# A decoder layer on one core: the first modulation's weights in three transfers, its last block taken into the column sums, and the squares of x's last rows ahead of a copy

## The chip, the cores and the metric

The kernel runs on one core of a Trainium2 chip. The metric is the device time of one execution in microseconds, lower is better. Two numbers appear: the time of an execution, and the span of a profiled execution, from the first to the last instruction that the profiler recorded.

## The reference, cut to what matters

The layer takes x (512 rows of 1024) and a condition vector c of 1024. Its start, which is what the change touches:

```python
mod = jax.nn.silu(c) @ w_ada + b_ada
shift, scale, gate = jnp.split(mod, 3, axis=-1)
h = rms_norm(x, norm_gain) * (1 + scale[:, None, :]) + shift[:, None, :]
proj = h @ w_in
```

`rms_norm` divides each row by the root of the mean of its squares and multiplies by a gain. `proj` then feeds a sliding-window attention group (A) and a native sparse attention group (B) with compressed, selected and window branches; both are gated by SiLU(z), joined, multiplied by `w_out`, gated and added to x.

## The kernel before, in words

The 1024 columns of h are worked through as 8 tiles of 128 (k = 0 to 7), and the 512 rows as 4 blocks of 128 (tb). For each k the kernel needs a shift and a scale for its 128 columns. It then forms h transposed (columns on partitions), splits it into a high and a low part (hh, hl), splits the weights likewise (swh, swl in the profile), and adds three products, `first_proj(k, 0..2)` at L309 and L310, into six PSUM banks (`pj_q` sq0 to sq3, `pj_kv` skv0 and skv1).

Before the first of these products (k = 0) the following happens, in an order written out by hand: the whole stretch stands in `with in_order(tc)`, which fixes each engine's order of instructions to that of the program. Names are those of the code; the profile drops the numbers behind them.

- SyncE (SP) issues the loads: x0 (the first 128 rows of x with small inputs), three more blocks of x, then the modulation weights of k = 0 (`load_ada(0)`, L221, `ada_ring`), the projection weights of k = 0 (`load_wst`, L225, `wst_ring`), and the same for k = 1 to 3 with a small transfer for the bias lines (L331) between. Each issue takes a place on this queue; from the ninth on an issue waits until the eighth before it has landed.
- TensorE turns x by 128 x 128 transposes into PSUM (`x_turned`, L341); VectorE (L372, L373) and, for the last block, ScalarE (L382, L383) copy the result to `xTp`. For block 2 the second half goes through the bank `pj_q[0]`. Dummy matmuls with zeros (`dummies`, L336) stand between; unless told otherwise they write `pj_q[0]`.
- ScalarE squares and sums the rows of x (L371, L376) and VectorE does so for half of the last block (L377). L379, L380 and `rsqrt` (L102 to L109) make the reciprocal roots, `rx`. They are transposed and spread over the partitions (L393, bank `rbp`), and `scaled` (L293) multiplies them into the turned x.
- The modulation of k = 0: `mod_pe` (L237) multiplies SiLU(c), eight columns of 128, with the weights: for each half e four blocks c, block 4e + c of the inputs, into four groups of 32 rows of the bank `pm`, of which one row each is not zero. ScalarE copies `pm` to `macc` (L241). `mod_col` (L247) sums over the rows with a column of ones into `pc`. `mod_ab` (L252, L253) makes shift and scale (AB) of it. `dummies(ND[3])`, two of them, stand between the two halves, and two more behind `mod_col`.
- ScalarE makes the projection weights' high part (`weights_high`, L285) and then h in three pieces (L404). The first L309 needs both.

The banks `pm`, `rbp` and `pc` are taken in this order from one pool of two buffers:

```python
ps_pj = ctx.enter_context(tc.tile_pool(name="ps_pj", bufs=2, space=PSUM))
```

The order around the modulation:

```python
first_mod = mod_pe(0)
next(first_mod)
dummies(ND[3])
for _ in first_mod:
    pass
rbp = ps_pj.tile([128, 512], F32, name="pj")
```

Behind this stage a loop over k runs the products while the next k's modulation, h and weights are made, and the attention and the output projection follow.

Of the kernel before, what the change touches and what calls it, by code (L numbers as in the profile page):

```python
# [19 lines left out]
S, D, HD, NB = 512, 1024, 64, 4  # L20
# [11 lines left out]
ND = (9, 0, 1, 2)  # L32
# [50 lines left out]
def hybrid_layer_kernel(ctx, tc, A, out):  # L83
    nc = tc.nc
    PE, DVE, ACT, POOL, SP = nc.tensor, nc.vector, nc.scalar, nc.gpsimd, nc.sync
# [12 lines left out]
    def rsqrt(v, n):  # L98

        y = sm.tile([128, n], F32, name="n_y")  # L100
        t = sm.tile([128, n], F32, name="n_t")
        DVE.tensor_scalar(y.bitcast(I32), v.bitcast(I32), -0.5, float(MAGIC), op0=OP.mult, op1=OP.add)  # L102
        DVE.tensor_tensor(t, y, y, op=OP.mult)
        DVE.scalar_tensor_tensor(t, t, -0.375 * NEWTON[0], v, op0=OP.mult, op1=OP.mult)
        DVE.scalar_tensor_tensor(y, t, 0.375 * NEWTON[0] * NEWTON[1], y, op0=OP.add, op1=OP.mult)
        DVE.tensor_tensor(t, y, y, op=OP.mult)
        DVE.scalar_tensor_tensor(t, t, 64.0 / 9.0, v, op0=OP.mult, op1=OP.mult)
        DVE.scalar_tensor_tensor(t, t, -10.0 / 3.0, t, op0=OP.add, op1=OP.mult)
        DVE.scalar_tensor_tensor(y, t, 5.0, y, op0=OP.add, op1=OP.mult)  # L109
        return y  # L110
# [13 lines left out]
    cT, prm, ident = first[:, 0:8], first[:, 8:40], first[:, 40:168]  # L124
# [8 lines left out]
    ones = con.tile([128, 1], F32, name="ones")  # L133
# [13 lines left out]
    sc_col = con.tile([128, 8], F32, name="sc_col")  # L147
# [66 lines left out]
    ada, wst = {}, {}  # L214
# [2 lines left out]

    def load_ada(k):
        ada[k] = ada_ring[:, k % NR]
        for e in range(2):  # L220
            SP.dma_start(ada[k][:, e], A["w_ada_ss"][k][:, e])  # L221

# [5 lines left out]
    macc, pcs = {}, {}  # L228
# [3 lines left out]
    def mod_pe(k):  # L232

        pm = ps_pj.tile([128, 512], F32, name="pj")[:, 0:256]
        for e in range(2):
            for c in range(4):
                PE.matmul(pm[32 * c:32 * c + 32, :], scz[:, 4 * e + c, :], ada[k][:, e, 256 * c:256 * c + 256],  # L237
                          start=e == 0, stop=e == 1, skip_group_check=True)
            yield
        macc[k] = stp.tile([128, 2, 128], F32, name="macc", bufs=2)  # L240
        ACT.activation(macc[k].rearrange("p a b -> p (a b)"), pm, AF.Copy)  # L241

    def mod_col(k):

        pc = pcs[k] = ps_pj.tile([128, 512], F32, name="pj")
        for s in range(2):
            PE.matmul(pc[:, s:s + 1], macc[k][:, s, :], ones, start=True, stop=True)  # L247

    def mod_ab(k):

        pc = pcs.pop(k)
        DVE.tensor_tensor(AB[:, k, 1:2], pc[:, 0:1], prm[:, k:k + 1], op=OP.add)  # L252
        DVE.scalar_tensor_tensor(AB[:, k, 0:1], pc[:, 1:2], prm1[:, k:k + 1], prm[:, 24 + k:25 + k],  # L253
                                 op0=OP.add, op1=OP.mult)
# [11 lines left out]
    pj_q = [spb.tile([128, 512], F32, name=f"sq{tb}") for tb in range(4)]  # L266
    pj_kv = [spb.tile([128, 2, 256], F32, name=f"skv{p}") for p in range(2)]
    flat_kv = [t.rearrange("p a b -> p (a b)") for t in pj_kv]
# [21 lines left out]
    def scaled(k, by, parts=(slice(0, S),)):  # L290
        y[k] = xT[k]
        for c in parts:
            DVE.tensor_tensor(y[k][:, c], xT[k][:, c], by[:, c], op=OP.mult)  # L293
# [19 lines left out]
    halves = (slice(0, 256), slice(256, 512))  # L313
    quarters = tuple(slice(128 * t, 128 * t + 128) for t in range(NB))

    with in_order(tc) as begun:
# [6 lines left out]
        for tb in range(1, NB):  # L323
            SP.dma_start(xn[:, tb], A["xn"][tb - 1])
        load_ada(0)
        load_wst(0)
        for k in range(1, NR):
            load_ada(k)
            load_wst(k)
            if k == 2:  # L330
                SP.dma_start(bl[0:48, :], A["bias"])  # L331
        DVE.memset(scz, 0.0)

        def dummies(n, bank=pj_q[0]):
            for _ in range(n):
                PE.matmul(bank, zero[:, 0:128], zero, start=True, stop=True)  # L336

        def x_turned(tb, bank, half=0):
            for k in range(4):
                c = 128 * (4 * half + k)  # L340
                PE.transpose(bank[:, 128 * k:128 * k + 128], xn[:, tb, c:c + 128], ident)  # L341

        def x_kept(tb, bank, half=0):
            return xTp[:, 4 * half:4 * half + 4, 128 * tb:128 * tb + 128], bank.rearrange("p (k q) -> p k q", k=4)
# [12 lines left out]
        def silu_rows(g):  # L357
            for j in range(4):
                PE.transpose(flat_kv[g][:, 128 * j:128 * j + 128],
                             sc_col[:, 4 * g + j:4 * g + j + 1].to_broadcast([128, 128]), ident)  # L360

        for tb in range(NB):
            dummies(ND[tb] if 0 < tb < 3 else 0, flat_kv[1])
            x_turned(tb, pj_q[tb])
            if tb < 3:
                x_turned(tb, (flat_kv[0], pj_q[3], pj_q[0])[tb], 1)
            if tb == 2:
                for g in range(2):
                    silu_rows(g)
            if tb < 3:  # L370
                ACT.activation(sqs, xn[:, tb], AF.Square, scale=1.0 / 32, accum_out=ss[:, tb:tb + 1])  # L371
                DVE.tensor_copy(*x_kept(tb, pj_q[tb]))  # L372
                DVE.tensor_copy(*x_kept(tb, (flat_kv[0], pj_q[3], pj_q[0])[tb], 1))  # L373
        x_turned(3, pj_q[2], 1)
        sx = con.tile([128, NB], F32, name="sx")
        ACT.activation(sqs[:, 0:512], xn[:, 3, 0:512], AF.Square, scale=1.0 / 32, accum_out=ss[:, 3:4])  # L376
# [2 lines left out]
        DVE.tensor_scalar(sx[:, 0:3], ss[:, 0:3], EPS, None, op0=OP.add)  # L379
        DVE.scalar_tensor_tensor(sx[:, 3:4], ss[:, 3:4], EPS, ss[:, 4:5], op0=OP.add, op1=OP.add)  # L380
        rx = rsqrt(sx, NB)
        ACT.activation(*x_kept(3, pj_q[3]), AF.Copy)  # L382
        ACT.activation(*x_kept(3, pj_q[2], 1), AF.Copy)  # L383
        for g in range(2):
            ACT.activation(scb[:, 512 * g:512 * g + 512], flat_kv[g], AF.Copy)
# [3 lines that stand above are left out]
        for _ in first_mod:  # L389
            pass  # L390
        rbp = ps_pj.tile([128, 512], F32, name="pj")
        for tb in range(NB):
            PE.transpose(rbp[:, tb * 128:(tb + 1) * 128], rx[:, tb:tb + 1].to_broadcast([128, 128]), ident)  # L393
        mod_col(0)
        dummies(ND[3])
        scaled(0, rbp, halves[0:1])
        mod_ab(0)
        scaled(0, rbp, halves[1:2])
        scaled(1, rbp)
# [33 lines left out]
        for k in range(8):  # L433
            if k + NR < 8:
                load_ada(k + NR)
                load_wst(k + NR)
            if k == LW - 1:
                SP.dma_start(rest[:, 0:960], A["rest"])
                for _ in range(5):
                    load_next()  # L440
            first_proj(k, 0)
            if k + 1 in PE_MOD:
                for _ in mod_pe(k + 1):
                    pass
            first_proj(k, 1)
            if k + 1 in PE_MOD:
                mod_col(k + 1)
            if k == 2:
                bank = ps_pj.tile([128, 512], F32, name="pj")
                bias_lines(bank)  # L450
            if k < 7:
                new_tile(k + 1)
            if k == 2:
                ACT.activation(lsb, bank[0:64, 0:320], AF.Copy)
                for a in range(2):
                    for b in range(2):
                        SP.dma_start(line_d[a, :, 320 * b:320 * b + 320], lsb[32 * b + 8 * a:32 * b + 8 * a + 8, :])
            first_proj(k, 2)
            if k == 7:
                split_to("kv_cmp", 3, 0)  # L460
# [38 lines left out]
    def PJ():  # L499
        n_pj[0] += 1  # L500
        return (ps_px if n_pj[0] % 3 == 0 else ps_pj).tile([128, 512], F32, name="pj")
# [577 lines left out]
    for n in range(8):  # L1079
# [3 lines left out]
        for c in halves if n == 7 else (slice(0, S),):  # L1083
            b = PJ()[:, 0:c.stop - c.start]
# [78 lines left out]
```

## Time and profile before

| what | us |
| --- | --- |
| median of three runs | 306.17 |
| the three runs | 306.03, 306.17, 306.64 |
| the profiled execution, its own time | 306.96 |
| its span | 305.2 |

A row of a timeline gives the start in us from the span's start, the time in us, engine, line, operation, what is written and what is read, and how many instructions are merged; in brackets stands the idle time of the engine before it and what ended that. PE is TensorE, PEld its weight loads, DVE VectorE, ACT ScalarE, SPq the queue that issues transfers. A matmul of 32-bit floats shows as two records: eight records of L237 are four matmuls. A row of the waits gives who waited for whom, the total in us, how often, and the longest.

### The profile page before, as it was taken

Reading aid. Unit: us, or ns where it says so; the run is one execution under the profiler, and the core shown is the slowest. Engines: PE = TensorE matmul, PEld = TensorE weight load, DVE = VectorE, ACT = ScalarE, POOL = GpSimd, SP = SyncE. Lnnn points to the kernel's source line nnn. Section 1 sums busy time; section 2 is a strip of 40 time slices with the busy share of each in tenths; the row PEclk is TensorE's granted clock in tenths of the full one; section 3 lists DMA queues with packets and bytes.
Section 4 is the critical chain, followed back from the end, with each engine's and each line's share of the span. In section 5 each row is a group of like instructions: output and inputs, shape, how many; then the busy total and the mean of one; then the engine's idle time right before and its main releaser. Section 6 shows DMA issues by size and latency. Waiting matters only on the chain.

```text
span 305.2 us, 5838 instructions
## 1 busy us (share of the span) xinstructions
PE 295.9 (97%) x2119; PEld 252.4 (83%) x2119; DVE 238.7 (78%) x668; ACT 195.6 (64%) x474; POOL 4.7 (2%) x26
## 2 busy tenths in 40 slices
PE   8999999999999999999999999999999999989994
PEld 4677888889989999989787887888888888868884
DVE  3899996999985587977999999999978958555321
ACT  4876547777975579958696677759767847623100
POOL 1000000000100000000000000000000000000000
PEclk9999999999999999999999999999999999999998
DMA  7999957893475650410815030545400000008331
GB/s 270 378 375 409 337 192 257 256 275 122 140 213 168 207 174 2 126 49 0 273 40 207 2 103 34 210 146 198 131 12 0 0 2 1 2 10 244 92 103 37
DMA packets 27420, 44.21 MB, mean 145 GB/s; under 512 B 1712, under 2 KB 19408, under 8 KB 27392
## 3 DMA queue, kind: packets, MB, share of 16 engines
q1 hardware_dynamic: 27392, 43.84, 42.9%
q8 instruction: 17, 0.28, 0.4%
q14 instruction: 11, 0.09, 0.1%
HBM read 41.70 MB, written 2.14 MB: 144 GB/s over the span
## 4 chain that ended last, share of the span: by engine, by line
PE 76%; DVE 10%; ACT 6%; DMA 3%; issue 2%; SPq 1%; ACTq 0%
PE pj L522 30%; PE sq L309 8%; PE po L1010 8%; PE s L932 6%; PE pj L512 6%; PE pt L993 4%; PE skv L310 4%; PE pt L983 3%; DMA ada_ring<-in_w_ada_ss 3%; PE s L639 2%; DVE wl L191 2%; DVE qs L572 1%; ACT qs L571 1%; DVE pa L940 1%; ACT pa L947 1%
## 5 line engine op out<-in xcount | busy, mean ns | idle before, releaser
L190 ACT ACTIVATE wh<-raw 128x512 fp32r<-128x512 f32 (+1 forms) x52 | 31.7, 632 | 22.1 <-PE pj L522 20.6
L191 DVE TENSOR_TENSOR wl<-raw,wh 128x512 fp32r<-128x512 f32 (+1 forms) x52 | 35.1, 692 | 6.8 <-ACT wh L190 6.4
L512 PE MATMUL pj<-wl,hh 128*128 128x256 f32 (+1 forms) x128 | 37.0, 289 | 0.0
L512 PE MATMUL pj<-wh,hh 128*128 128x256 f32 (+1 forms) x128 | 36.5, 287 | 0.0
L512 PE MATMUL pj<-wh,hl 128*128 128x256 f32 (+1 forms) x128 | 36.3, 285 | 0.0
L947 ACT ACTIVATE pp<-pp,nm 128x256 f32<-128x256 f32 (+2 forms) x48 | 29.3, 611 | 7.2 <-DVE nm L940 7.0
L522 PE MATMUL pj<-hh,wh 128*128 128x512 f32 x80 | 32.2, 403 | 0.0
L522 PE MATMUL pj<-hl,wh 128*128 128x512 f32 x80 | 31.9, 399 | 0.0
L522 PE MATMUL pj<-hh,wl 128*128 128x512 f32 x80 | 31.6, 395 | 0.0
L940 DVE CUSTOM_DVE_ANT_0 pp<-s,bias 128x256 f32<-128x256 f32 (+2 forms) x48 | 25.9, 552 | 2.2 <-PE s L932 1.7
L522 PE MATMUL pj<-yh,wh 128*128 128x512 f32 (+1 forms) x72 | 26.2, 373 | 1.3 <-ACT yh L869 1.3
L522 PE MATMUL pj<-yh,wl 128*128 128x512 f32 (+1 forms) x72 | 26.9, 373 | 0.0
L522 PE MATMUL pj<-yl,wh 128*128 128x512 f32 (+1 forms) x72 | 26.9, 373 | 0.0
L1010 PE MATMUL po<-ptT,xf 128*64 128x128 f32 x432 | 25.3, 274 | 0.0
L1010 PEld LDWEIGHTS po<-ptT,xf 128*64 128x64 f32 x432 | 23.5, 137 | 1.5 <-issue 0.9
L512 PEld LDWEIGHTS pj<-wl,hh 128*128 128x128 f32 x128 | 24.1, 188 | 0.3 <-issue 0.2
L512 PEld LDWEIGHTS pj<-wh,hl 128*128 128x128 f32 x128 | 24.1, 188 | 0.3 <-issue 0.3
L512 PEld LDWEIGHTS pj<-wh,hh 128*128 128x128 f32 x128 | 24.1, 189 | 0.2 <-issue 0.2
L932 PE MATMUL s<-kTb,qs 128*128 128x256 f32 (+2 forms) x96 | 23.5, 357 | 0.0
L968 DVE TENSOR_SCALAR pp<-pp,rr,xf 128x256 f32<-128x256 f32 (+2 forms) x48 | 21.2, 477 | 0.5
L994 ACT COPY ptT<-pt 128x384 f32<-128x384 f32 (+1 forms) x32 | 16.2, 524 | 4.7 <-PE pt L993 3.1
L947 ACT ACTIVATE pa<-pa,nm 128x257 f32<-128x257 f32 (+1 forms) x32 | 15.2, 476 | 4.1 <-DVE nm L940 4.1
(241 smaller groups left out, 676.0 us busy)
## 6 DMA issues: line engine op xcount, KB each, us to landing
ada_ring<-in_w_ada_ss SPq DMA_DIRECT2D x16, 512.0 KB, 10.0
raw<-in_w_cmp SPq DMA_DIRECT2D x8, 512.0 KB, 5.3
raw<-in_w_gate SPq DMA_DIRECT2D x8, 512.0 KB, 4.4
raw<-in_w_o SPq DMA_DIRECT2D x8, 512.0 KB, 4.6
wst_ring<-in_w_qkv_a SPq DMA_DIRECT2D x8, 384.0 KB, 9.7
xr<-in_xT SPq DMA_DIRECT2D x8, 256.0 KB, 3.1
bias<-line_d SPq DMA_DIRECT2D x8, 256.0 KB, 3.9
raw<-in_w_q_b SPq DMA_DIRECT2D x4, 512.0 KB, 5.1
```

The source lines that it names most:

```text
L190: ACT.activation(wh, src, AF.Copy)
L191: DVE.tensor_tensor(wl, src, wh.bitcast(F32), op=OP.subtract)
L309: PE.matmul(pj_q[tb], lt, w[:, 0:512], start=f, stop=l, skip_group_check=True)
L310: PE.matmul(pj_kv[tb // 2][:, tb % 2, :], lt, w[:, 512:768], start=f and tb % 2 == 0, stop=l, skip_group_check=True)
L512: PE.matmul(bank[:, t * n:(t + 1) * n], h[:, tb * 128:(tb + 1) * 128], w[:, k % 2, :], start=k == 0 and m == 0, stop=k == 7 and m == 2)
L522: PE.matmul(bank, w, h[:, cols], start=k == 0 and m == 0, stop=k == 7 and m == 2)
L932: PE.matmul(ps[g], qs[h][:, 128 * i:128 * i + 128], kT[br, g][:, hl_, lo:lo + n], start=hl_ == 0, stop=hl_ == 1)
L940: DVE.tensor_tensor_reduce(out=P[:, g, 0:w], in0=ps[g][:, 0:w], in1=bt, scale=1.0, scalar=init, op0=OP.add, op1=OP.min, accum_out=nm[:, g: ...
L947: ACT.activation(P[:, g, 0:e], P[:, g, 0:e], AF.Exp, bias=nm[:, g:g + 1], scale=-1.0, accum_out=dn[:, g:g + 1])
L968: DVE.tensor_scalar(v, v, rr[:, g:g + 1], gates[:, g, br:br + 1], op0=OP.mult, op1=OP.mult)
L994: ACT.copy(T[:, 0:nb, :], rev(pt[:, 0:nb * 128].rearrange("p (b q) -> p b q", b=nb)))
L1010: PE.matmul(o[64 * g:64 * g + 64, 128 * i:128 * i + 128], vb[:, 64 * g:64 * g + 64], sl["T"][g][:, b, :], start=first_of and b == 0, stop= ...
```

## The change

The modulation weights of k = 0 come in three transfers instead of two: columns 0 to 1024 (half 0), 1024 to 1792 (three blocks of half 1) and 1792 to 2048 (its last block). The row products leave out the last block. `mod_col(0)` multiplies it with its column of SiLU(c) straight into the column sums, ahead of the sums of `macc`. The root's transposes are split: two blocks and the first half of `scaled` stand before `mod_col(0)`, two blocks after, and one dummy fewer follows. The copy of block 2's second half out of `pj_q[0]` moves behind `rsqrt`, so VectorE's squares of x's last rows come before it.

```diff
     def load_ada(k):
         ada[k] = ada_ring[:, k % NR]
+        if k == 0:
+            flat = lambda t: t.rearrange("p a b -> p (a b)")
+            for lo, hi in ((0, 1024), (1024, 1792), (1792, 2048)):
+                SP.dma_start(flat(ada[k])[:, lo:hi], flat(A["w_ada_ss"][k])[:, lo:hi])
+            return
         for e in range(2):
             SP.dma_start(ada[k][:, e], A["w_ada_ss"][k][:, e])
...
         for e in range(2):
-            for c in range(4):
+            for c in range(3 if e and k == 0 else 4):
                 PE.matmul(pm[32 * c:32 * c + 32, :], scz[:, 4 * e + c, :], ada[k][:, e, 256 * c:256 * c + 256],
                           start=e == 0, stop=e == 1, skip_group_check=True)
...
         pc = pcs[k] = ps_pj.tile([128, 512], F32, name="pj")
+        for s in range(2 if k == 0 else 0):
+            PE.matmul(pc[:, s:s + 1], ada[k][:, 1, 768 + 128 * s:896 + 128 * s], sc_col[:, 7:8], start=s == 0, stop=False,
+                      skip_group_check=True)
         for s in range(2):
-            PE.matmul(pc[:, s:s + 1], macc[k][:, s, :], ones, start=True, stop=True)
+            PE.matmul(pc[:, s:s + 1], macc[k][:, s, :], ones, start=k > 0, stop=True, skip_group_check=True)
...
                 DVE.tensor_copy(*x_kept(tb, pj_q[tb]))
-                DVE.tensor_copy(*x_kept(tb, (flat_kv[0], pj_q[3], pj_q[0])[tb], 1))
+                if tb < 2:
+                    DVE.tensor_copy(*x_kept(tb, (flat_kv[0], pj_q[3])[tb], 1))
...
         rx = rsqrt(sx, NB)
+        DVE.tensor_copy(*x_kept(2, pj_q[0], 1))
         ACT.activation(*x_kept(3, pj_q[3]), AF.Copy)
...
         rbp = ps_pj.tile([128, 512], F32, name="pj")
-        for tb in range(NB):
-            PE.transpose(rbp[:, tb * 128:(tb + 1) * 128], rx[:, tb:tb + 1].to_broadcast([128, 128]), ident)
+
+        def root_turned(tbs):
+            for tb in tbs:
+                PE.transpose(rbp[:, tb * 128:(tb + 1) * 128], rx[:, tb:tb + 1].to_broadcast([128, 128]), ident)
+
+        root_turned((0, 1))
+        scaled(0, rbp, halves[0:1])
         mod_col(0)
-        dummies(ND[3])
-        scaled(0, rbp, halves[0:1])
+        root_turned((2, 3))
+        dummies(ND[3] - 1)
         mod_ab(0)
         scaled(0, rbp, halves[1:2])
         scaled(1, rbp)
```

## The prediction

> **What bounds the kernel now.** I read the page's first part, then the chain of work that ended last in order of time, then the timeline of each engine between 8 and 17 us, where the edited lines run, and last who waited for whom on TensorE.
>
> ```profile
> span 305.2 us, 5838 instructions
> PE 295.9 (97%) x2119; PEld 252.4 (83%) x2119; DVE 238.7 (78%) x668; ACT 195.6 (64%) x474; POOL 4.7 (2%) x26
> ```
>
> The chain in order of time, from the weights of the first modulation to the first matmul of the projection:
>
> ```profile
> 3.35 8.41 DMA ada_ring<-in_w_ada_ss
> 11.80 0.64 PE pj L237 x8
> 12.44 0.58 PE pj L393 x4
> 13.02 0.59 PE pj L247 x4
> 13.96 0.50 ACT hh L404
> 14.50 0.50 PE sq L309
> ```
>
> Behind 14.50, TensorE's waits up to 60 us come to one entry, the one that ends there:
>
> ```profile
> PE sq L309 <- ACT hh L404: 0.4, 1, 0.4
> ```
>
> So the start waits on data, and from 14.5 us the kernel is a stream of matmuls almost without holes. A microsecond won or lost before 14.5 us therefore arrives at the end nearly whole. The question is when the first L309 starts. Before it stand: the weights land (11.76 by the chain), the second half of the row products (L237), ScalarE's copy of them (macc), the column sums (L247), two small VectorE steps (L252, L253), h (L404).
>
> TensorE and ScalarE there:
>
> ```profile
> 11.14 0.60 PE L336 MATMUL sq<-zero 128*128 128x512 bf16 x2
> 11.80 0.64 PE L237 MATMUL pj<-ada_ring,scz 128*32 128x256 f32 x8
> 12.37 0.65 PE L393 MATMUL pj<-xf,n_y 128*128 128x128 f32 x4
> 12.99 0.61 PE L247 MATMUL pj<-ones,macc 128*128 128x1 f32 x4
> ...
> 9.10 0.63 ACT L376 ACTIVATE sq_both<-xf 128x512 f32<-128x512 f32 x1
> 9.63 0.19 ACT L376 ACTIVATION_READ_ACCUMULATOR sq_both<-xf 128x1 f32 x1
> ...
> 11.18 1.09 ACT L385 ACTIVATE xf<-skv 128x512 f32<-128x512 f32 x2
> 12.56 0.38 ACT L241 ACTIVATE macc<-pj 128x256 f32<-128x256 f32 x1 [0.28 <-PE pj L237]
> 12.84 0.83 ACT L285 ACTIVATE swh<-wst_ring 128x768 fp32r<-128x768 f32 x1
> 13.96 0.88 ACT L404 ACTIVATE hh<-xTp,AB 128x128 fp32r<-128x128 f32 x2 [0.28 <-DVE AB L253]
> ```
>
> VectorE there:
>
> ```profile
> 9.14 0.68 DVE L373 COPY xTp<-sq 128x512 f32<-128x512 f32 x1
> 9.73 0.68 DVE L377 CUSTOM_DVE_ANT_0 sq_both<-xf 128x512 f32<-128x512 f32 x1
> ...
> 10.53 0.16 DVE L380 SCALAR_TENSOR_TENSOR sx<-ss 128x1 f32<-128x1 f32 x1
> ...
> 12.11 0.16 DVE L109 SCALAR_TENSOR_TENSOR n_y<-n_t,n_y 128x4 f32<-128x4 f32 x1
> 13.06 0.42 DVE L293 TENSOR_TENSOR xTp<-xTp,pj 128x256 f32<-128x256 f32 x1 [0.79 <-PE pj L393]
> 13.64 0.16 DVE L252 TENSOR_TENSOR AB<-pj,xf 128x1 f32<-128x1 f32 x1 [0.15 <-PE pj L247]
> 13.71 0.21 DVE L253 SCALAR_TENSOR_TENSOR AB<-pj,prm,xf 128x1 f32<-128x1 f32 x1
> 13.84 1.01 DVE L293 TENSOR_TENSOR xTp<-xTp,pj 128x256 f32<-128x256 f32 x2
> ```
>
> **The change part by part.**
>
> *The squares ahead of the copy.* The copy at 9.14 leaves its place and L377 takes it: x's last rows are there (ScalarE squares them from 9.10), and the ScalarE sum that L380 needs ends at 9.82. So L377 and all behind it move up by 9.73 - 9.14 = 0.59: L109 starts at 11.52 and ends at 11.68. The copy follows, 0.08 before L109's end by the overlap of neighbours that don't depend on each other (13.71 + 0.21 against 13.84), so from 11.60 to 12.28. VectorE's next work, L293, starts later than that before and after, so VectorE itself loses nothing.
>
> *Who waits for the moved copy.* It reads the PSUM bank `pj_q[0]`, and the two dummy matmuls between the halves of the first modulation write that bank by default (`sq<-zero` at 11.14). Before, the copy ended at 9.82, long ahead of 11.14. Now it ends at 12.28, it stands ahead of the dummies in the program, and a matmul that overwrites a bank waits for its reader, as elsewhere in this trace:
>
> ```profile
> PEld pt L993 <- ACT ptT L994: 0.3, 1, 0.3
> ```
>
> TensorE's order is fixed, so the second half of the products, the transposes of the root and the column sums are queued behind the dummies. From the end of a VectorE step to TensorE it is 0.10 (L109 ends at 12.27, L393 starts at 12.37): dummies from 12.38 to 12.98.
>
> ```profile
> 16.07 0.28 PE L310 MATMUL skv<-swh,hh 128*128 128x256 f32 x1
> 16.27 1.07 PE L237 MATMUL pj<-ada_ring,scz 128*32 128x256 f32 x16
> ```
>
> L237 here starts 0.08 before the full-width matmul ahead of it ends, so the second half starts at 12.90 instead of 11.80: 1.10 later. Bounds: 12.80 if a dummy only holds the array for its stream, and 13.00 if the copy starts after L109 has ended. I take 12.90, since L310 then L237 is the same pair of shapes.
>
> *Three blocks of four.* Sixteen records take 1.07 and eight 0.64, so one is 0.054 and six take 0.53: the products end at 13.43 (bounds 0.38 less or 0.64). ScalarE's copy follows by 0.12 as before (12.44 to 12.56): macc from 13.55 to 13.93. ScalarE had the L385 copies until 12.27, so that is no longer what it waits on. The weights' high part (0.83) follows until 14.66 and is hidden until h is due.
>
> *Root transposes first, then the sums.* Four take 0.65; two, 0.12 apart, 0.41. They run from 13.35 to 13.76, inside the wait for macc, and release the first half of L293 at 13.80, which ends at 14.22. Hidden, since h needs AB later than that.
>
> *The last block into the column sums.* The column sums as records:
>
> ```profile
> L247 PE MATMUL pj<-ones,macc x8: 166/250/271, 13.0 to 19.0; 128*128 128x1 f32 x8
> ```
>
> Two matmuls of this form are added, four records, spaced (0.61 - 0.25) / 3 = 0.12. Written to run before macc is there, they can't: the tile `pc` is the third from a pool of two buffers, so it takes the bank of `pm`, which macc is copied from. They wait for that copy (13.93), and L247 starts 0.05 after it (12.94 to 12.99), at 13.98. Eight records instead of four then take 0.25 + 7 x 0.12 = 1.09 and end at 15.07 instead of 13.60. Bounds: 14.60 if the four direct ones were hidden ahead of macc, and 15.20 if the four cost a whole 0.61 more.
>
> *Behind them.* L252 starts 0.04 after the sums: 15.11 instead of 13.64; L253 and h follow as before: h at 15.43, first L309 at 15.97. The other two transposes, 0.41, end by 15.4 and the second half of L293 starts some 0.07 late, which its reader covers: the third L404 piece comes two pieces, 0.88, after the first. One dummy fewer saves nothing, since the two ran while L309 waited for h.
>
> *Three transfers instead of two.* The queue that issues transfers, SyncE's:
>
> ```profile
> 2.87 0.96 SPq L221 DMA_DIRECT2D ada_ring<-in_w_ada_ss  x2
> 3.88 0.44 SPq L225 DMA_DIRECT2D wst_ring<-in_w_qkv_a  x1
> ...
> 10.54 0.33 SPq L225 DMA_DIRECT2D wst_ring<-in_w_qkv_a  x1
> 11.84 0.34 SPq L331 DMA_DIRECT2D raw<-in_bias  x1
> 12.74 2.15 SPq L221 DMA_DIRECT2D ada_ring<-in_w_ada_ss  x2
> ```
>
> One issue more is 0.48 on this queue, covered by the 8.4 us between issue and landing. The steps at 10.54, 11.84 and 12.74 are each let go by the landing of the eighth transfer before, so the landings lie 1.30 (512 KB) and 0.90 (384 KB) apart: the extra transfer shows no gap of its own. At that pace the 384 KB piece lands near 11.5 and the last 128 KB near 11.85, both long before 12.90 and 13.98. The next five issues now wait for one transfer earlier in the line, the last of them (bias) at about the old time; their data are used from 16.3 us on, later now, so nothing is exposed. If it were, a late weight stalls ScalarE first.
>
> The Trainium skill, page "DMA: Bandwidth & Descriptors", gives each transfer a fixed cost of about 2 us, mostly the receipt of the last byte. These landings, 0.90 and 1.30 apart, show no such gap between queued transfers. Were it paid in series, the first projection weights would land near 14.7, their high part end near 15.6 instead of 14.66, and the sum would be 0.15 us more.
>
> **The sum.** 15.97 - 14.50 = +1.47 us: +1.10 (dummies wait) - 0.11 (six records for eight) + 0.48 (direct matmuls behind macc). This is made against the profiled execution, 306.96 us with its span of 305.2; the median of the runs is 306.17, 0.79 below it, and 306.17 + 1.47 = 307.6. Ends of the terms: (1.00 - 0.26 + 0) = +0.74 and (1.20 + 0 + 0.60) = +1.80, so 306.9 to 308.0.
>
> **The rivals.**
>
> *The dummies don't wait (not slower).* The point is whether the copy ends before TensorE reaches them at 11.14; by the chain above it ends at 12.28, so it would need to be 1.1 us earlier, or the bank's reader not waited for. Then the second half starts at the end of the dummies, 11.66, ends at 12.20, macc starts when ScalarE is free at 12.28 (0.28 earlier than before) and ends at 12.66, and eight records end at 13.80 against 13.60: +0.2, or with the direct ones ahead of macc 13.32 and -0.28. That is 305.9 to 306.4. For it: nothing in the rows; against it: the program's order and the bank. Chance 0.13.
>
> *The direct matmuls are hidden ahead of macc.* Dummies wait, bank free: +0.99, 307.2. For it: rows don't show bank reuse here. Chance 0.12.
>
> *TensorE's clock falls.* A hole opens from 11.2 to 12.4, and the column sums are tiny.
>
> ```profile
> 1.23 4.02 PE L336 MATMUL sq<-zero 128*128 128x512 bf16 x9 [1.23 <-DVE ada_ring L320]
> ...
> 300.56 0.28 PE L522 MATMUL pj<-yh,wl 128*128 128x256 f32 x1
> ...
> 302.00:303.00 1.00, 0.00 (x0) 0.00 (x0) 0.00 (x0) 0.00 (x0) 0.00 (x0) 1.00 0.35 124
> 303.00:304.00 1.00, 0.00 (x0) 0.00 (x0) 0.00 (x0) 0.00 (x0) 0.00 (x0) 0.50 0.04 7
> ```
>
> At the end TensorE stops at 300.84 and the granted clock is 0.50 from 303.0, after 2.2 us of rest. Nine dummies took 4.02 at the start, 0.45 each, and two took 0.60 later. The new hole is 1.2 us, with 0.22 and then 0.25 us more within the next 3 us. If it is enough, some 2 to 3.4 us of matmuls behind 15.97 run at half speed and cost 1.0 to 1.7 more: 308.6 to 309.3. Chance 0.10.
>
> The Trainium skill, page "TensorE: Matmul & The Clock Gate", Part 1, says that the clock is halved after an idle window of about 3.4 us. By it the hole is too short; the trace's end shows that 2.2 us of rest can do, so the case keeps its chance.
>
> *A late small transfer or a late weight.* Up to another 0.8 on the sum, 308.4. Chance 0.05.
>
> **How the numbers follow.** The forecast itself has 0.60. A difference within 0.2%, 0.6 us, is about what this kernel's runs can't tell from none (306.03 to 306.64). Slower by more than that: forecast, hidden direct matmuls, clock, late transfer, 0.87, less 0.02 for a sum at its lower end in a low run: 0.85. The first rival and that 0.02 make 0.15, of which 0.03 stand beyond the bound on the faster side (its -0.28 with the spread of the runs) and 0.12 within it. Range: forecast and second rival (0.72) lie in 306.9 to 308.0; upward it takes in the late transfer and half of the clock case, to 309.0; it leaves out the first rival. With 0.1 for the spread of runs: 306.8 to 309.0.
>
> **What would show it.** Right: the L336 pair between the two L237 groups starts near 12.4 and names the L391 copy of xTp as what it waited for; second L237 group, six records, at 12.9; macc at 13.55; L247 and the direct matmuls together behind macc, ending near 15.1; first L309 near 16.0; L109 near 11.5; the span about 306.7. Wrong: dummies still at 11.14; direct matmuls ahead of macc; a granted clock of 0.50 after 12 us; or new waits of L309 behind 16 us that give time back or add to it.

## The result, and the profile after

The changed kernel takes 307.62 us in the median (306.72 to 309.64, eight executions) and the kernel before 305.99 (305.49 to 306.64, eight): a ratio of 1.0062, 95% interval 1.0035 to 1.0088. It is slower, by about 1.6 us.

That median stands between two groups. Each execution has a mean granted TensorE clock. Four executions of the changed kernel have 1.000 and take 306.72 to 307.29 (median 306.89). The other four have 0.991 to 0.994 and take 307.94 to 309.64 (median 308.81). An interval of 3.41 us at half speed gives a mean of 1 - 1.71 / 305 = 0.994, and the end of an execution can add to it. The 81 executions of the kernel before that were timed beside the experiments have 0.996 or more. So two things are to be explained: about 0.9 us in every execution, and about 1.9 us in half of them.

The profile shown is of an execution with a full clock: its own time is 306.72, its span 304.9. That span is a little shorter than the 305.2 of the profile before, although the first product comes later in it; the part on the prediction says where the difference goes. First the span and the engines of the page, then TensorE's timeline from the dummies to the first product, VectorE's and ScalarE's. The lines have moved: L336 is L344, L237 is L242, L393 is L405, L247 is L252 (direct) and L255 (macc), L404 is L419, L309 is L317. Two dummies stand in the program where the first row shows one; the other left no record.

```profile
span 304.9 us, 5843 instructions
PE 295.2 (97%) x2119; PEld 251.9 (83%) x2120; DVE 238.8 (78%) x668; ACT 195.5 (64%) x474; POOL 4.7 (2%) x26
```

```profile
12.22 0.38 PE L344 MATMUL sq<-zero 128*128 128x512 bf16 x1 [0.87 <-DVE xTp L391]
12.75 0.63 PE L242 MATMUL pj<-ada_ring,scz 128*32 128x256 f32 x6
13.31 0.43 PE L405 MATMUL pj<-xf,n_y 128*128 128x128 f32 x2
13.92 0.60 PE L252 MATMUL pj<-sc_col,ada_ring 128*128 128x1 f32 x4 [0.18 <-ACT macc L246]
14.39 0.58 PE L255 MATMUL pj<-ones,macc 128*128 128x1 f32 x4
15.88 0.50 PE L317 MATMUL sq<-swh,hh 128*128 128x512 f32 x1 [0.42 <-ACT hh L419]
...
9.04 0.68 DVE L386 CUSTOM_DVE_ANT_0 sq_both<-xf 128x512 f32<-128x512 f32 x1
11.40 0.16 DVE L109 SCALAR_TENSOR_TENSOR n_y<-n_t,n_y 128x4 f32<-128x4 f32 x1
11.49 0.69 DVE L391 COPY xTp<-sq 128x512 f32<-128x512 f32 x1
15.01 0.16 DVE L260 TENSOR_TENSOR AB<-pj,xf 128x1 f32<-128x1 f32 x1 [0.81 <-PE pj L255]
...
13.48 0.38 ACT L246 ACTIVATE macc<-pj 128x256 f32<-128x256 f32 x1 [1.25 <-issue]
15.33 0.88 ACT L419 ACTIVATE hh<-xTp,AB 128x128 fp32r<-128x128 f32 x2 [0.73 <-DVE AB L261]
```

The root's last step starts 0.71 us sooner (11.40 against 12.11), and nothing profits: the moved copy runs from 11.49 to 12.18, and the first row names it as what the dummies waited for, 0.87 us. The second row products start at 12.75 instead of 11.80, the direct matmuls wait for macc, and the first product starts at 15.88 instead of 14.50.

### The profile page after: what moved, and what is told of

Same layout as the page of the kernel before. It is cut to its first block, busy times and chain, and to the rows that moved or that the text cites. A ratio compares the mean times of both kernels' runs of the same rounds, so it can differ in the third digit from the quotient of the medians.

```text
span 304.9 us, 5843 instructions
## 1 busy us (share of the span) xinstructions
PE 295.2 (97%) x2119; PEld 251.9 (83%) x2120; DVE 238.8 (78%) x668; ACT 195.5 (64%) x474; POOL 4.7 (2%) x26
## 4 chain that ended last, share of the span: by engine, by line
PE 76%; DVE 12%; ACT 6%; issue 2%; DMA 2%; SPq 0%; ACTq 0%
PE pj L537 30%; PE sq L317 8%; PE po L1025 8%; PE s L947 6%; PE pj L527 6%; PE pt L1008 4%; PE skv L318 4%; PE pt L998 3%; PE s L654 2%; DMA xf<-in_xn 2%; DVE wl L191 2%; DVE qs L587 1%; ACT qs L586 1%; DVE pa L955 1%; ACT pa L962 1%
```

## The experiments

All times are compared with the kernel before on the same chip. "First product" is the start of the first L309 or L317 in the profiled execution. It moves by half a microsecond from one execution to the next with the landing of the weights (14.50 and 14.01 in two profiles of the kernel before), so the path is read by its steps, and the time by medians. The step used below goes from the start of the second row products to the first product: 14.50 - 11.80 = 2.70 us before, 15.88 - 12.75 = 3.13 in the changed kernel.

**The copy alone.** The kernel before, with one edit:

```diff
-                DVE.tensor_copy(*x_kept(tb, (flat_kv[0], pj_q[3], pj_q[0])[tb], 1))
+                if tb < 2:
+                    DVE.tensor_copy(*x_kept(tb, (flat_kv[0], pj_q[3])[tb], 1))
...
         rx = rsqrt(sx, NB)
+        DVE.tensor_copy(*x_kept(2, pj_q[0], 1))
```

> The kernel before, with the moved copy as the only edit. Theory (dummies wait): dummies near 12.3, second L237 group of eight near 12.85, first product near 15.5, 1.0 us behind before; 306.9 in executions at full clock, and part of the executions 1.7 us above that with a lower granted clock. Rival (the copy's place is harmless, the rest of the change costs): within 0.3 us of before, one clock.

Measured: 307.13 us (306.73 to 307.53, six) against 305.90, ratio 1.0042 (1.0025 to 1.0058). TensorE's timeline:

```profile
12.33 0.38 PE L336 MATMUL sq<-zero 128*128 128x512 bf16 x1 [1.16 <-DVE xTp L383]
12.85 0.64 PE L237 MATMUL pj<-ada_ring,scz 128*32 128x256 f32 x8
15.55 0.50 PE L309 MATMUL sq<-swh,hh 128*128 128x512 f32 x1 [0.45 <-ACT hh L406]
```

The wait is there, 1.16 us, the second products start 1.05 later than in the first profile of before and so does the first product; the step between them is 2.70, as before. The move alone makes the kernel slower. But none of its six executions has a clock below 1.000, although its hole on TensorE is longer than the changed kernel's. The second half of the expectation fell.

**The dummies in a free bank.** The changed kernel with

```diff
-        dummies(ND[3])
+        dummies(ND[3], pj_q[1])
```

between the halves.

> The changed kernel, with the two dummies between the halves of the first modulation written to a bank whose readers are long done (sq1 instead of sq0). Theory (the dummies' wait for the moved copy costs 1.1 us, and the hole it leaves on TensorE lets the granted clock fall in part of the executions, 1.7 us each): dummies near 11.3 instead of 12.22, second L242 group near 11.8, macc limited by ScalarE from about 12.3, first product near 14.7 instead of 15.88; the median within 0.4 us of before, and no execution with a granted clock below that of the others. Rival (the loss comes from the three transfers and the direct matmuls): first product at 15.4 or later, 306.7 or more, and the slow executions stay.

Measured: 306.42 us (305.57 to 308.67, twelve) against 305.90, ratio 1.0022 (1.0001 to 1.0044). Two of twelve have a clock of 0.994; the other ten have a median of 306.25. TensorE and ScalarE:

```profile
11.48 0.38 PE L344 MATMUL sq<-zero 128*128 128x512 bf16 x1 [0.16 <-issue]
11.79 0.63 PE L242 MATMUL pj<-ada_ring,scz 128*32 128x256 f32 x6
12.96 0.61 PE L252 MATMUL pj<-sc_col,ada_ring 128*128 128x1 f32 x4 [0.18 <-ACT macc L246]
13.66 0.84 ACT L293 ACTIVATE swh<-wst_ring 128x768 fp32r<-128x768 f32 x1 [0.75 <-DMA wst_ring<-in_w_qkv_a]
14.94 0.50 PE L317 MATMUL sq<-swh,hh 128*128 128x512 f32 x1 [0.44 <-ACT hh L419]
```

The wait is gone and most of the loss with it, though the profiled execution is not at the expected 14.7: the projection weights landed late there, and ScalarE waited 0.75 for them until 13.66. The fall of the clock stays, in two of twelve executions, where none was expected.

**The rest without the copy's move.** The changed kernel with the copy in its old place.

> The changed kernel, with the copy back in its old place; transfers, three blocks, direct matmuls and split transposes as changed. Theory: no wait of the dummies; the root is ready at 12.27 as before, macc from 12.3 to 12.7, eight records of column sums behind it and behind the transposes, first product near 14.8, 0.3 us behind before: 306.0 to 306.4, no fall of the clock. Rival (the rest costs): 306.7 or more.

Measured: 306.62 us (305.73 to 308.31, twelve), ratio 1.0023 (1.0003 to 1.0043); first product at 14.80. Five of twelve have a clock of 0.992 to 0.994 and a median of 307.39, the other seven 306.17. The path came out as expected, 0.3 over before; the clock fell, against the expectation, though the dummies did not wait.

**The column sums in a bank of their own**, once with the dummies in the free bank and once with the dummies waiting. The edit of both:

```diff
-        pc = pcs[k] = ps_pj.tile([128, 512], F32, name="pj")
+        pc = pcs[k] = ps_pj.tile([128, 512], F32, name="pj") if k else pj_q[1]
```

> As the run with the dummies in a free bank, and the column sums of k = 0 also go to bank sq1 instead of to the bank that macc is copied from. Theory (the direct matmuls wait for macc only because of the bank): they run before macc is there, the sums of macc end near 13.3, first product near 14.25, 0.3 us ahead of before and 0.45 ahead of the run without own bank; 305.5 to 305.9. Rival (the direct matmuls cost nothing where they are, being short): no difference between the two runs, 306.2.

> The changed kernel with the column sums of k = 0 in bank sq1 instead of the bank that macc is copied from; the dummies still wait. Theory (bank reuse puts the direct matmuls behind macc): they run at about 13.6 ahead of macc's end, first product near 15.4 instead of 15.88, 0.5 us less than the changed kernel in executions at full clock, 306.4. Rival (their place costs nothing): first product stays at 15.9.

Measured, dummies in the free bank: 305.94 us (305.18 to 307.35, twelve) against 305.90, ratio 1.0007 (0.9989 to 1.0024), no fall. Dummies waiting: 306.93 us (306.55 to 308.47, twelve) against 306.17, ratio 1.0032 (1.0018 to 1.0046); one of twelve at 0.990, the others 306.90 in the median, where 306.4 was expected. TensorE's timeline with the dummies in the free bank:

```profile
11.45 0.63 PE L242 MATMUL pj<-ada_ring,scz 128*32 128x256 f32 x6
12.02 0.43 PE L405 MATMUL pj<-xf,n_y 128*128 128x128 f32 x2
12.29 0.51 PE L252 MATMUL sq<-sc_col,ada_ring 128*128 128x1 f32 x4
14.14 0.50 PE L317 MATMUL sq<-swh,hh 128*128 128x512 f32 x1 [0.42 <-ACT hh L419]
```

and with the dummies waiting:

```profile
12.44 0.38 PE L344 MATMUL sq<-zero 128*128 128x512 bf16 x1 [1.08 <-DVE xTp L391]
13.79 0.50 PE L252 MATMUL sq<-sc_col,ada_ring 128*128 128x1 f32 x4
15.64 0.50 PE L317 MATMUL sq<-swh,hh 128*128 128x512 f32 x1 [0.41 <-ACT hh L419]
```

In both, L252 follows the transposes at once and waits for nothing. From the waiting dummies to the first product it is 15.64 - 12.44 = 3.20 us, against 15.88 - 12.22 = 3.66 with the shared bank: bank reuse cost 0.46. With both waits gone, the first product comes 0.36 ahead of the first profile of before. But the path is not shorter than before: the step from the second row products is 14.14 - 11.45 = 2.69, against 2.70. The 0.36 comes from a second half that started sooner, 11.45 against 11.80, and in its second profile the kernel before starts it at 11.31. So without its two waits these profiles show no gain from the rest of the change, and the time, 305.94 against 305.90, shows none either.

**What lets the clock fall.** Two theories stood: the hole ahead of the second products, or thin work on TensorE later, up to the first product. The hole filled (changed kernel, `dummies(4, pj_q[1])` ahead of the two that wait):

> The changed kernel with four more dummies, in the free bank sq1, ahead of the two that wait: TensorE works through the hole of 0.87 us, and the path stays as it is. Executions of the changed kernel fall in two groups, 306.7 to 307.3 at a mean granted clock of 1.000 and 307.9 to 309.6 at 0.991 to 0.994. Theory A (the hole lets the clock fall): no execution below 0.996, all at 306.7 to 307.4. Theory B (what lets it fall is the thin work on TensorE between 12.7 and 15.9: three blocks instead of four, column sums of one column each, one dummy): the hole has little part, and a third or so of the executions still show 0.991 to 0.994.

The kernel before with both pairs of dummies, between the halves and behind the sums, left out:

> The kernel before, without the two dummies between the halves and without the two behind the column sums; nothing else. Both theories: first product at 14.50 as before. Theory B (thin work on TensorE lets the clock fall): a third or more of the executions at 0.995 or less and 1.7 us above the others, though no wait is added, the others at 305 to 306.5. Theory A (a hole of about 0.9 us or more is needed): the hole from 11.2 to 11.8 is too short, all executions as before.

The kernel with the copy in its old place, and `dummies(ND[3] + 1)` instead of `dummies(ND[3] - 1)`:

> The changed kernel with the copy in its old place, and three dummies instead of one behind the last root transposes, where TensorE waits for h. With one, 5 of 12 executions had a clock of 0.994 or less. Theory B (thin work between the second row products and the first product lets the clock fall): first product stays near 14.8, the executions at 0.994 or less become rare or vanish, the median falls from 306.6 to 306.2. Theory A (something else, as a wait, lets it fall): as many as with one dummy.

The changed kernel with the same three dummies:

> The changed kernel with three dummies instead of one behind the last root transposes. Theory (the changed kernel is two things: a path some 0.9 us longer in every execution, and a fall of the clock for 3.4 us in half of them, because TensorE has too little to stream ahead of the first product): no execution with a clock of 0.995 or less, median 306.8 to 307.1, all within 0.8 us of each other. Rival (the fall has to do with the waits, which all stay): a third or more of the executions at 0.994 or less, 307.6 in the median.

All kernels, with the dummies that stand behind the column sums or the last transposes:

| kernel | dummies there | executions | of them at 0.995 or less | their median us | median us of the others |
| --- | --- | --- | --- | --- | --- |
| before | 2 | 81 | 0 | none | 305.75 to 306.17 by chip |
| the copy alone | 2 | 6 | 0 | none | 307.13 |
| free bank, own bank, two dummies (below) | 2 | 12 | 0 | none | 305.67 |
| changed | 1 | 8 | 4 | 308.81 | 306.89 |
| hole filled | 1 | 6 | 6 | 308.57 | none |
| copy in its old place | 1 | 12 | 5 | 307.39 | 306.17 |
| dummies in a free bank | 1 | 12 | 2 | 308.03 | 306.25 |
| free bank, own bank | 1 | 12 | 0 | none | 305.94 |
| own bank | 1 | 12 | 1 | 308.47 | 306.90 |
| before without dummies | 0 | 12 | 4 | 306.90 | 305.81 |
| copy in its old place, three dummies | 3 | 12 | 0 | none | 306.14 |
| changed, three dummies | 3 | 12 | 2 | 308.25 | 307.23 |

The ratios to before: hole filled 1.0079 (1.0061 to 1.0096), before without dummies 0.9995 (0.9980 to 1.0010), three dummies with the copy in its old place 0.9994 (0.9982 to 1.0005), three dummies in the changed kernel 1.0043 (1.0024 to 1.0062). The first product came at 16.00 with the hole filled, at 14.54 in before without dummies, at 15.24 with the copy in its old place and three dummies, and at 16.00 in the changed kernel with three. Only the 15.24 is far from what was expected, 14.8, and there the second half landed late (its products start at 12.11); the step is 3.13, as with one dummy.

Two of these profiles caught a fall. The stretches of the run with the hole filled; behind a stretch and its length stand the busy times of PE, PEld, DVE, ACT and POOL, and the third figure from the end is the granted clock:

```profile
13.14:16.55 3.41, 2.82 (x22) 1.81 (x17) 1.77 (x6) 2.21 (x5) 0.00 (x0) 1.00 1.03 414
16.55:19.96 3.41, 3.41 (x23) 1.88 (x22) 3.35 (x5) 2.19 (x4) 0.00 (x0) 0.50 1.04 367
19.96:23.40 3.44, 3.44 (x27) 2.88 (x20) 1.54 (x4) 1.23 (x3) 0.00 (x0) 1.00 1.00 373
```

And of before without dummies:

```profile
11.10:14.51 3.41, 2.08 (x24) 1.09 (x16) 2.39 (x12) 3.05 (x7) 0.00 (x0) 1.00 1.00 392
14.51:17.92 3.41, 3.38 (x16) 2.42 (x20) 3.23 (x5) 2.77 (x5) 0.00 (x0) 0.50 1.03 419
```

The clock is at 0.50 for 3.41 us, while the first products run. With the hole filled, all six executions fell, and the copy alone has the longer hole and none fell, so the hole is not the cause. Before without its dummies falls in four of twelve, with no wait added and nothing moved. Two more dummies ahead of the first product take the falls from five of twelve to none where the copy is in its old place (median 306.62 to 306.14), and from four of eight to two of twelve in the changed kernel, so there it is less than expected, and such a difference can be chance. The first pair was also timed on two chips, and the second pair at two times. Over the table, none of 99 executions with two dummies there fell, and 18 of 62 with one. But with one dummy it was 17 of 38 where the column sums share the bank of macc, and 1 of 24 where they have their own. So the dummies behind the column sums have a part in holding the clock, and they are not all of it.

**The changed kernel and the kernel before once more**, unaltered, one profile each.

> The changed kernel unaltered, for a second profile. In ten profiles the 124 matmuls from the 93rd behind the first product take either 21.5 or 21.9 us, and nothing between. If this is a matter of the program, this one takes 21.5 as in the first profile of the changed kernel; if of the execution, it can take 21.9. First product near 15.9 in either case.

> The kernel before, unaltered, for a second profile. By the program: the same stretch takes 21.9 again; by the execution: it can take 21.5. First product near 14.5.

Measured, one execution each: 310.19 us with a clock of 0.993, and 306.01. The changed kernel's stretches:

```profile
10.37:13.78 3.41, 1.98 (x20) 0.73 (x20) 1.91 (x9) 2.02 (x4) 0.00 (x0) 1.00 0.98 366
13.78:17.19 3.41, 2.82 (x18) 1.91 (x18) 2.18 (x6) 2.62 (x6) 0.00 (x0) 1.00 1.03 419
17.19:20.61 3.42, 3.42 (x22) 1.63 (x21) 3.33 (x5) 1.79 (x3) 0.00 (x0) 0.50 1.03 340
```

This is the changed kernel's own fall, at 17.19. The stretch with the hole (1.98 us busy) is not followed by it; the fuller one behind it (2.82 us) is. The first product was at 16.23 here and at 14.01 in the second profile of before: neither is as near to the first profiles as expected. The steps are the same as in the first profiles, 16.23 - 13.10 = 3.13 and, by the rows of before, 14.01 - 11.31 = 2.70:

```profile
11.31 0.64 PE L237 MATMUL pj<-ada_ring,scz 128*32 128x256 f32 x8
14.01 0.50 PE L309 MATMUL sq<-swh,hh 128*128 128x512 f32 x1 [0.45 <-ACT hh L404]
```

The stretch of 124 matmuls took 21.50 us in the changed kernel and 21.58 in the kernel before, which had 21.91 in its first profile. So it belongs to the execution, not to the program.

**A version without either wait.** Free bank, own bank for the sums, two dummies instead of one behind the last transposes.

> The kernel of the run with free bank and own bank for the column sums, with two dummies instead of one behind the last root transposes. Theory (path 0.36 us shorter than before at the first product, nothing else changed behind it): 305.6 to 305.9, no execution with a granted clock of 0.995 or less. Rival (what is won at the start is lost behind it): 305.9 to 306.3, no different from before.

Measured: 305.67 us (305.02 to 306.03, twelve) against 305.75, ratio 0.9986 (0.9967 to 1.0005), none below 0.998. The median lies in the theory's range, but the kernel before is as low on this chip, and by the interval the two can't be told apart: the rival is what was seen. ScalarE and TensorE:

```profile
13.38 0.84 ACT L293 ACTIVATE swh<-wst_ring 128x768 fp32r<-128x768 f32 x1 [0.69 <-DMA wst_ring<-in_w_qkv_a]
14.67 0.50 PE L317 MATMUL sq<-swh,hh 128*128 128x512 f32 x1 [0.61 <-ACT hh L419]
```

In this execution the projection weights are what comes last: macc ends at 12.69, and ScalarE then waits 0.69 for them, until 13.38; in the changed kernel's first profile they land at 12.94. Here the transfer behind the modulation's decides.

## Why the prediction was right or wrong, point by point

The time, 307.6, is the measured median within 0.02, and that is partly luck. The sum stood for a full clock, where the changed kernel takes 306.89 (four executions) and, with three dummies, 307.23 against 305.75 (ten). That is 0.9 to 1.5 us over before, against the 1.47 of the sum. The rest of the measured difference is the clock, a rival with a chance of 0.10; a granted clock of 0.50 after 12 us, one of the prediction's own signs of being wrong, came in half of the executions. The two terms that carry the sum, the dummies' wait and the shared bank, are shown on the path each by a run that takes it away.

- **Squares ahead of the copy**: L109 forecast at 11.52, measured 11.40. Right.
- **The dummies wait for the copy**: forecast 12.38, measured 12.22, and 12.33 with the copy alone. The step of 1.10 measured 0.95 in the changed kernel and 1.05 with the copy alone, both against the 11.80 of the first profile of before. Right.
- **Three blocks of four save 0.11**: wrong. Six records took 0.63 us and eight 0.64, so the term is worth 0.01. Each record lasts 0.38 to 0.40 us, and six are done in 0.63: the blocks run side by side, and one less shortens nothing.
- **Direct matmuls behind macc, 0.48**: the bank is what they waited for, and taking it away is worth 0.46. Right.
- **First product**: forecast 15.97, measured 15.88, +1.38 to the first profile of before against +1.47. Of it 0.95 lies ahead of the second row products and 0.43 behind their start.
- **Three transfers cost nothing**: SyncE's rows, let go by landings as before:

```profile
10.69 0.33 SPq L226 DMA_DIRECT2D ada_ring<-in_w_ada_ss  x1
11.62 0.33 SPq L230 DMA_DIRECT2D wst_ring<-in_w_qkv_a  x1
12.07 0.36 SPq L339 DMA_DIRECT2D raw<-in_bias  x1
12.96 0.35 SPq L226 DMA_DIRECT2D ada_ring<-in_w_ada_ss  x1
```

  The pieces land at 10.67, 11.61, 11.96 and the projection weights at 12.94, against 11.5 and 11.85 forecast for the two later pieces. Right. The Trainium skill ("DMA: Bandwidth & Descriptors", section "Anatomy of one DMA — SWDGE (gpsimd) path") gives a transfer a fixed cost of about 2 us, fitted on that path. These are issued by SyncE, and no gap of that size stands between them: the last two pieces land 0.35 us apart.
- **One dummy fewer saves nothing**: this is a step that failed. It was weighed for the path only, and there it holds. For the clock it does not: over the table above it falls in 18 of 62 executions with one dummy and in none of 99 with two. That one dummy fewer is the whole reason is not shown.
- **The clock rival**: its size was right. The first 44 matmuls took 7.66 us in the second profile of the changed kernel and 6.13 in the first, 1.5 more, against 1.0 to 1.7. Its reason was wrong in the main: it was put down to the hole, with the thin column sums beside it. And its chance was too small: it came in half of the executions. The Trainium skill's rule ("TensorE: Matmul & The Clock Gate", Part 1), an idle window of about 3.4 us, spoke against it; the length of the fall, 3.41 us, agrees with the page's window, but the stretch ahead of it had 2.82 us of work, not none.

In the first profiles of the two kernels the difference can be followed to the end. It is 1.38 at the first product. The stretch of 124 matmuls gives 0.41 of it back (21.50 against 21.91) and the others together less than 0.1, so the last matmul starts 0.90 later, at 301.46 against the 300.56 of before:

```profile
301.46 0.28 PE L537 MATMUL pj<-yh,wl 128*128 128x256 f32 x1
```

From there to the end of the span it is about 3.5 us in this profile and 4.6 in the one of before, so the changed kernel's span comes out shorter. Both differences go with the execution as far as the profiles show: the stretch differs between the two profiles of before (21.91 and 21.58), and the end takes 5.0 in the changed kernel's second profile. The 0.9 in the medians, from four executions against eight, is therefore no close measure of the path. Where the stretch takes the same 21.91, with the copy alone, the 1.05 of the first product is still 1.06 at the last matmul, so what is lost at the start does arrive whole, as the prediction said.

## What to carry to other kernels

When a read of a buffer is moved later, look for every writer of that buffer in the stretch it now crosses, dummies and their default arguments too: here an operand meant for nothing held the path for a microsecond. A bank taken from a small pool is a wait on the reader of its last user, so work written ahead of that reader does not run ahead of it. Filler work that looks free on the path can have a part in holding the clock: judge its removal over many executions and by their granted clock, since one profile can show either case. And an earlier first product in one profile is not a shorter path: compare the step from an event that both kernels share.

## What the runs showed that I had not expected

The granted clock falls for one interval of 3.41 us after a stretch in which TensorE was busy for 2.82 of 3.41 us by the records, and does not fall after one with 1.98 (both in the second profile of the changed kernel). So neither the length of a hole nor the busy share tells when it falls.

An estimate from the fourteen traces does better. Count only the time in which columns stream, by the spacing of like matmuls that follow each other at once: 0.21 us for a dummy, 0.11 for a 32-bit record of 128 columns, 0.24 for records of 256 columns side by side in 32-column groups, 0.45 ns a column for the rest, and nothing for matmuls of one column, though each of their records lasts 0.25 us. The traces' own entries of the clock put every change a whole number of 3.41 us intervals behind its rise to full, and that rise comes between 4.27 and 7.00 us. The 17 intervals that end with a fall, those at the end of the kernel included, hold at most about 1.3 us of such streaming; the 1200 others at full clock hold about 1.3 or more. Of the two of the changed kernel above, the one with the fall holds 1.31 and the other 1.51.

By the same count, with the dummies that left no record added, the poorest 3.41 us near the first product, wherever an interval may begin, holds 0.9 to 1.3 us in the seven kernels of which executions fell, and 1.36 to 1.75 in the five of which none did. That would explain why one kernel falls in some executions only: an interval has to lie over the poor stretch. The count was fitted after the runs, on one or two profiles of each kernel, and no run was made to test it. Why all six executions with the hole filled fell stays open.

A stretch of the same matmuls runs at two paces. VectorE and ScalarE do the same work there, and the clock is full. TensorE's groups between 29.1 and 51 us in the first profile of before (count, busy time, mean ns of one):

```profile
L309 PE MATMUL sq<-swh,hl 128*128 128x512 f32 x23 | 8.4, 399 | 0.0
L310 PE MATMUL skv<-swh,hl 128*128 128x256 f32 x23 | 6.5, 281 | 0.0
```

and between 28.6 and 50.5 us in its second:

```profile
L309 PE MATMUL sq<-swh,hl 128*128 128x512 f32 x23 | 8.3, 394 | 0.0
L310 PE MATMUL skv<-swh,hl 128*128 128x256 f32 x23 | 6.4, 278 | 0.0
```

In fourteen profiles the 124 matmuls took 21.91 us in seven, 21.50 in five and 21.58 in two; the other stretches I compared agree within 0.15, the 44 matmuls in which a fall lies aside. These 0.4 us go with the execution, and their cause was not looked into.
